# A two-layer diffusion backbone on one core: gate transposes by DMA in the later FFNs, and two modulation streams at other times and rates

## The chip, the cores and the metric

The program runs on one core of a Trainium2 chip. TensorE (PE) multiplies, VectorE (DVE), ScalarE (ACT) and GpSimd (POOL) work on tiles in on-chip memory, SyncE (SP) issues nearly all transfers. The metric is the device time of one execution in microseconds, as the median of several runs. One execution of the kernel was recorded by the hardware profiler; all rows quoted here are from it.

## What is computed

The program runs two layers over 256 latent tokens and 256 context tokens of width 1024, in float32. Each layer is a gated FFN of half weight, a mixer and another such FFN; the mixer is neighbourhood attention in layer 0 and a short gated convolution in layer 1. Each sub-layer has a shift, a scale and a gate from a modulation vector, a product of the conditioning vector with `ada_w`.

```python
def swiglu_ffn(h, w_in, w_out):
    a, u = jnp.split(h @ w_in, 2, axis=-1)        # w_in: 1024 x 5632
    return (jax.nn.silu(a) * u) @ w_out           # w_out: 2816 x 1024

def half_step_ffn(x, shift, scale, gate, w_in, w_out, g, b):
    y = swiglu_ffn(modulate(x, shift, scale), w_in, w_out)
    return post_norm_update(x, y, gate, 0.5, g, b)   # layer_norm(alpha*x + 0.5*gate*y)

m = (s_c @ ada_w[i] + ada_b[i]).reshape(B, N_MOD, 1, D)   # nine vectors per layer
```

After the attention only the latent tokens go on. What is left then is the second FFN of layer 0, written FFN(0,1), then FFN(1,0), the convolution (products `wc` and `wo`), and FFN(1,1). These three FFNs are where the change works.

## The kernel before

**Products.** Every matrix is split in a high part, rounded to the float32r type, and a low part that holds the rest. A product is then three matmuls: high by high and high by low (lines 165 and 166 of the kernel, in `mmu`), low by high (line 168). One call of `mmu` takes two 128-row blocks of the contraction, so six matmuls with 512 columns. The text calls it a chunk. After each chunk `tick` moves a clock on by one, and everything that is put off is counted in these chunks.

**Weights.** `wunit` loads 512 KB of weights (a unit) into one of four raw buffers on SP's queue. ScalarE rounds it to the high part (line 211, in two halves) and VectorE subtracts to the low part (line 214, in two halves). There are five buffers for the high part and five for the low part, and in the last phase `ext[0]` more of each, from tags `whx` and `wlx`: three, so eight in all.

**w1 of an FFN.** `panels` runs over 11 panels of 256 gate and 256 up columns. A panel has four units and two token tiles of 128 tokens, eight chunks. The end of a token tile's panel is `gated.done`: ScalarE applies silu (line 494), VectorE multiplies by the up half (line 495, tile `sil`). Four chunks later (`Late(G_LAG, rest)`) TensorE transposes the two token tiles' results in four 128x128 pieces into a PSUM tile `gT` (line 503), and `finish` splits that into `gh` on ScalarE (line 113) and `gl` on VectorE (line 114). These are the left operands of w2.

**w2 of an FFN.** `out_gemm` goes through 22 units (11 for each half of the 1024 output columns). `order_skew` lets the second token tile follow the first by `LEAD` = 5 units, so in the steady part each unit of progress is two chunks. At the end of each output tile the residual and the norm's statistics run on VectorE (lines 402 to 409).

**Modulation streams.** `stream` and `ada` produce the vectors that later sub-layers need, in the background: 16 steps for two vectors, each step one 512 KB load `ar` (line 316) and, one step later, an addition on VectorE in two halves (tile `acc`, line 297; the first step of a vector is a plain product). The additions are held behind the last gate multiplication that was issued (`gate_ins`). When a vector's eight steps are done, GpSimd adds over the partitions (line 307) and a small accumulating DMA adds the sum into a scratch row in memory (line 308). Later SP loads such rows as `mrow` (line 376), which waits for that DMA. `set_background(gen, rate, hold)` emits `rate` steps per chunk after `hold` chunks; `drain` emits what is left at once, at the place in the program where it stands. The name (1, 4) below is vector 4 of layer 1.

**What sets the order.** TensorE's order is that of the program text. The other engines' orders are planned from it when the program is built. On every engine instructions run in their queue's order. In FFN(0,1) the stream for (1,4) and (1,5) runs beside w1 at 0.35 after 20 chunks, in FFN(1,0) that of (1,6) and (1,7) at 0.25 from the start, and both are drained after w1. In FFN(1,1) and the weights around it a stream of one vector, (1,8), runs at 0.15.

Of the kernel before, what the change touches and what calls it, by code (L numbers as in the profile page):

```python
# [9 lines left out]

F32 = mybir.dt.float32
F32R = mybir.dt.float32r
AF = mybir.ActivationFunctionType
ALU = mybir.AluOpType
AX = mybir.AxisListType
# [2 lines left out]
P = 128  # L18
# [7 lines left out]
NP = FF // 256  # L26
# [26 lines left out]
LT_LAG = (5, 5)  # L53
F0_LAG = (5, 5, 6, 7)
G_LAG = 4
ROPE_EARLY = 70
S_EARLY = 40
V_LAG = 1
# [3 lines left out]
W_HI = 2  # L62
# [2 lines left out]
ZP = ((0, 0), (1, 0), (0, 1), (0, 2), (1, 1), (1, 2))  # L65
E0 = (0,)
E2 = (0, 5, 7)
HOLD = 20


@with_exitstack
def backbone_kernel(
# [6 lines left out]
    nc = tc.nc  # L79
    sync = nc.sync  # L80
# [4 lines left out]
    sp = ctx.enter_context(tc.tile_pool(name="sp", bufs=2))  # L85
# [4 lines left out]

    uid = [0]
    w_early = [0]
    ext = [1, 0]
    ada_late = [0]

    def nm(s):
        uid[0] += 1
        return f"{s}_{uid[0]}"
# [54 lines left out]
    def set_background(gen, rate, hold=0):  # L153

        background[:] = [gen, rate, -rate * hold]

    def drain():
        while background[0] is not None:
            bg_step()
# [20 lines left out]
    def wunit(srcs, kn, s, own=None, wd=512, put_off=False):  # L180

        raw = wp.tile([P, UN], F32, tag="wr", bufs=WB[0], name=nm(s + "r"))
        if own:
            hs, ls = ([act(F32R, s + c) for _ in range(kn)] for c in "hl")
            rv = raw[:, :kn * 512].rearrange("p (a b) -> p a b", a=kn)
            with tc.high_priority(offset=w_early[0]):
                for src, c in srcs:
                    sync.dma_start(rv[:, :, c:c + src.shape[2]], src)  # L190
                for i in range(kn):
                    with queued(own[i]):
                        nc.scalar.activation(hs[i], rv[:, i], AF.Copy)
                        nc.vector.tensor_tensor(out=ls[i], in0=rv[:, i], in1=hs[i].bitcast(F32), op=ALU.subtract)
            return Parts(hs), Parts(ls)
        ext[1] += 1
        if ext[0] and ext[1] % (5 + ext[0]) in (E0 if ext[0] == 1 else E2):
            hi = hp.tile([P, UN], F32R, tag="whx", bufs=ext[0], name=nm(s + "h"))
            lo = hp.tile([P, UN], F32R, tag="wlx", bufs=ext[0], name=nm(s + "l"))
        else:  # L200
            hi = wp.tile([P, UN], F32R, tag="wh", bufs=WB[1], name=nm(s + "h"))
            lo = wp.tile([P, UN], F32R, tag="wl", bufs=WB[2], name=nm(s + "l"))
        rv, hv, lv = (t[:, :kn * wd].rearrange("p (a b) -> p a b", a=kn) for t in (raw, hi, lo))
        with tc.high_priority(offset=w_early[0]):
            for src, c in srcs:
                sync.dma_start(rv[:, :, c:c + src.shape[2]], src)

        def parts():
            m = kn * wd
            for a in range(0, m, m // W_HI):  # L210
                nc.scalar.activation(hi[:, a:a + m // W_HI], raw[:, a:a + m // W_HI], AF.Copy)  # L211
            for a in range(0, m, m // W_LO):
                b = a + m // W_LO
                nc.vector.tensor_tensor(out=lo[:, a:b], in0=raw[:, a:b], in1=hi[:, a:b].bitcast(F32), op=ALU.subtract)  # L214
            return hv, lv

        if put_off:
            return parts
        with tc.high_priority(offset=w_early[0]):
            return parts()  # L220
# [131 lines left out]
    def stream(*groups):  # L352
        for g in groups:
            yield from ada(g)
            made[0] += 1
            if made[0] == ADA_SLOW:
                background[1] = ADA_FAST
# [100 lines left out]
    def lead_in(np):  # L458

        r = range(KU)  # L460
        o = [(0, 0, u) for u in r] + [(0, 1, u) for u in r[:2]] + [(1, 0, u) for u in r] + [(1, 1, u) for u in r[:2]]
        o += [(t, 1, u) for u in r[2:] for t in range(2)]
        return o + [(t, p, u) for p in range(2, np) for u in r for t in range(2)]
# [20 lines left out]
    def run(gen):  # L484
        for _ in gen:
            pass

    def gated(func, finish, s):

        part, res = {}, []  # L490

        def done(p, t, bk):
            g = sp.tile([P, 256], F32, tag="s2", bufs=S2, name=nm("sil"))
            nc.scalar.activation(g, bk[:, 0:256], func)
            gate_ins[:] = [nc.vector.tensor_tensor(out=g, in0=g, in1=bk[:, 256:512], op=ALU.mult)]
            part[p, t] = g
            if t == 1:
                def rest():
                    ps = tpb(s)
                    for i in range(2):  # L500
                        g = part.pop((p, i))
                        for j in range(2):
                            nc.tensor.transpose(ps[:, j * 256 + i * P:j * 256 + (i + 1) * P], g[:, j * P:(j + 1) * P], ident)  # L503
                    return finish(p, ps)
                res.append(Late(G_LAG, rest))

        return done, res
# [325 lines left out]
    def lhs_T(tl):  # L833
        def f(k, t):
            s = (k % 2) * 256 + t * P
            g = tl[k // 2]
            hi, lo = g.get() if isinstance(g, Late) else g
            return hi[:, s:s + P], lo[:, s:s + P]
        return f

    def ffn(hTs, later, l, j, i, gm, nxt, own=()):
        def finish(p, ps):
            hi, lo = act(F32R, "gh"), act(F32R, "gl")
            split(ps, hi, lo)
            return hi, lo

        done, gT = gated(AF.Silu, finish, "gT")

        def done2(p, t, bk):
            done(p, t, bk)  # L850
            if p == 1 and t == 1:
                later()

        run(panels([(p * 256, FF + p * 256) for p in range(NP)], ffn_w_in[l, j], hTs, lead_in(NP), done2, "w1", own))
        drain()
        g, hTs, later = sub_end(ffn_w_out[l, j], lhs_T(gT), 2 * NP, l, i, gm, 0.5, nxt, "w2",
                                order_skew(NP) if nxt else order_last(NP))
        run(g)
        return hTs, later
# [263 lines left out]
    hp = phase.__enter__()  # L1123
    on_pool[0] = True
    sync.dma_start(scr[1][0, 4 * D:9 * D].rearrange("(a b) -> a b", a=16), ada_b[1, 4 * D:9 * D].rearrange("(a b) -> a b", a=16))
    ext[0] = 3

    set_background(stream([(1, 4, 0), (1, 5, 0)]), 0.35, HOLD)
    hTs, later = ffn(hTs, later, 0, 1, 2, 8, (1, 0), own)

    set_background(stream([(1, 6, 0), (1, 7, 0)]), 0.25)
    hTs, later = ffn(hTs, later, 1, 0, 0, 2, (1, 3))


    srow = cp.tile([24, P], F32, tag="row", name="srow")
# [52 lines left out]

    cols = [(0, 256), (512, 768)] + [(D + n * 256, 2 * D + n * 256) for n in range(4)]
    run(panels(cols, w, hTs, lead_in(6), done, "wc"))  # L1190
    g, hTs, later = sub_end(sc_w_out[0], lhs_T(yT), KC, 1, 1, 5, 1.0, (1, 6), "wo", order_late(KU))
    run(g)
    set_background(stream([(1, 8, 0)]), 0.15)
# [55 lines left out]
```

## Time and profile before

| | |
|---|---|
| median of three runs | 1257.53 us (1256.62 to 1257.73) |
| the profiled execution | 1258.45 us, of which the span of its records is 1256.7 us |
| mean granted TensorE clock | 0.998 |
| TensorE busy | 1241.4 us, 99% of the span |
| VectorE busy | 966.5 us, 77% |
| ScalarE busy | 590.2 us, 47% |

The stages can be told from the matmuls' operands. All times are in us from the span's start; the shares are worked out from one row per stage of a view by windows.

| stage | from, to | TensorE | VectorE | ScalarE | DMA share |
|---|---|---|---|---|---|
| FFN(0,0), both kinds of tokens | 0, 320 | 99% | 79% | 30% | 0.81 |
| attention | 320, 591 | 99% | 79% | 57% | 0.52 |
| FFN(0,1) w1 | 591, 718 | 99% | 88% | 58% | 0.87 |
| FFN(0,1) w2 | 718, 780 | 100% | 54% | 41% | 0.51 |
| FFN(1,0) w1 | 780, 906 | 100% | 87% | 57% | 0.82 |
| FFN(1,0) w2 | 906, 968 | 100% | 54% | 41% | 0.52 |
| convolution, wc and wo | 968, 1062 | 100% | 81% | 55% | 0.62 |
| FFN(1,1) w1 | 1062, 1188 | 99% | 78% | 58% | 0.71 |
| FFN(1,1) w2, end | 1188, 1256 | 90% | 53% | 27% | 0.38 |

How to read the rows in the next part: a timeline row has the start, the duration, the engine, the kernel's line, the operation, the tile written and those read, shapes, and in brackets how long the engine was idle before and what released it. In a row of groups the busy time and the mean in ns come after the first bar, the idle time and its releasers after the second. A row of waits has the waiting line, the releaser, the total in us, the count and the longest. SPq is SyncE's queue. `DMA share` is the mean busy share of 16 DMA engines.

### The profile page before, as it was taken

The numbers are of one execution on the slowest core, as the hardware profiler recorded it, in microseconds if no ns is written. First come the engines' busy times: TensorE is split into PE (matmuls) and PEld (weight loads), VectorE is DVE, ScalarE is ACT, GpSimd is POOL, SyncE is SP. The second block draws the span as 40 slices with busy tenths as digits, with TensorE's granted clock in tenths as the row PEclk, the third lists the DMA queues.
The fourth block names the chain that finished last, engine by engine and source line by source line (L and its number), as shares of the span: only waits on it lengthen the run. The fifth ranks groups of instructions, "written<-read, shape, count | busy, mean of one in ns | idle before, by whom it ended". The sixth has DMA issues, their size and how long they took to land.

```text
span 1256.7 us, 17284 instructions
## 1 busy us (share of the span) xinstructions
PE 1241.4 (99%) x5902; PEld 1006.9 (80%) x5902; DVE 966.5 (77%) x1675; ACT 590.2 (47%) x1152; POOL 85.0 (7%) x83
## 2 busy tenths in 40 slices
PE   8999999999999999999999999999999999999997
PEld 6787778778878878777888888888888887888886
DVE  3599987888878877789899646998646788878546
ACT  2432132312326556688655435655435744655431
POOL 0000000000001111120003100021100000002000
PEclk9999999999999999999999999999999999999999
DMA  9976678788842744455899645889645764885641
GB/s 308 299 235 226 197 236 290 265 260 274 285 156 85 216 94 87 99 115 179 259 335 318 231 150 167 274 293 321 224 146 167 245 206 134 259 290 185 227 159 53
DMA packets 202928, 268.59 MB, mean 214 GB/s; under 512 B 30246, under 2 KB 149534, under 8 KB 202840
## 3 DMA queue, kind: packets, MB, share of 16 engines
q1 hardware_dynamic: 202644, 267.46, 67.4%
q8 instruction: 46, 0.75, 0.2%
q14 instruction: 42, 0.34, 0.1%
q0 software_dynamic: 160, 0.02, 0.0%
q10 hardware_dynamic: 36, 0.02, 0.0%
HBM read 265.27 MB, written 2.20 MB: 213 GB/s over the span
## 4 chain that ended last, share of the span: by engine, by line
PE 92%; ACT 3%; DVE 3%; issue 1%; DMA 1%; POOL 0%; DVEq 0%; SPq 0%; POOLq 0%; ACTq 0%
PE f L695 19%; PE w L165 17%; PE w L168 17%; PE w L166 17%; PE wkv L165 2%; PE wkv L166 2%; PE wkv L168 2%; PE wc L165 2%; PE wc L168 2%; PE wc L166 2%; PE gT L503 1%; PE ada L624 1%; PE hT L437 1%; PE S L987 1%; PE wo L165 1%
## 5 line engine op out<-in xcount | busy, mean ns | idle before, releaser
L211 ACT ACTIVATE w1h<-w1r 128x512 fp32r<-128x512 f32 (+1 forms) x352 | 200.0, 620 | 180.0 <-PE w L168 81.5
L214 DVE TENSOR_TENSOR w1l<-w1r,w1h 128x512 fp32r<-128x512 f32 (+1 forms) x352 | 241.7, 734 | 35.5 <-ACT w1h L211 33.2
L165 PE MATMUL w<-w1h,hTh 128*128 128x512 f32 x528 | 209.1, 396 | 1.3 <-ACT hTh L113 1.3
L166 PE MATMUL w<-w1l,hTh 128*128 128x512 f32 x528 | 205.9, 390 | 0.3 <-DVE w1l L214 0.3
L297 DVE SCALAR_TENSOR_TENSOR acc<-ar,cst,acc 128x512 f32<-128x512 f32 x266 | 186.2, 747 | 15.3 <-DMA ar<-in_ada_w_dram 15.3
L165 PE MATMUL w<-w2h,gh 128*128 128x512 f32 (+1 forms) x446 | 173.4, 389 | 0.0
L166 PE MATMUL w<-w2l,gh 128*128 128x512 f32 (+1 forms) x446 | 172.1, 387 | 0.0
L211 ACT ACTIVATE w2h<-w2r 128x512 fp32r<-128x512 f32 x176 | 101.5, 624 | 145.2 <-PE w L168 106.5
L214 DVE TENSOR_TENSOR w2l<-w2r,w2h 128x512 fp32r<-128x512 f32 x176 | 114.1, 688 | 72.0 <-ACT w2h L211 71.2
L168 PE MATMUL w<-w1h,hTl 128*128 128x512 f32 x528 | 163.1, 390 | 0.2 <-DVE hTl L114 0.2
L168 PE MATMUL w<-w2h,gl 128*128 128x512 f32 (+1 forms) x446 | 136.1, 386 | 0.0
L695 PE MATMUL f<-h0h,w1h 128*128 128x512 f32 x352 | 133.1, 394 | 0.4 <-DVE h0h L650 0.4
L695 PE MATMUL f<-h0l,w1h 128*128 128x512 f32 x352 | 133.2, 391 | 0.0
L695 PE MATMUL f<-h0h,w1l 128*128 128x512 f32 x352 | 132.7, 390 | 0.0
L165 PEld LDWEIGHTS w<-w1h,hTh 128*128 128x128 f32 x528 | 99.2, 188 | 21.8 <-ACT hTh L113 2.1
L168 PEld LDWEIGHTS w<-w1h,hTl 128*128 128x128 f32 x528 | 98.9, 188 | 22.0 <-DVE hTl L114 1.0
L166 PEld LDWEIGHTS w<-w1l,hTh 128*128 128x128 f32 x528 | 99.2, 188 | 20.4 <-DVE w1l L214 0.7
L165 PEld LDWEIGHTS w<-w2h,gh 128*128 128x128 f32 x446 | 83.8, 188 | 19.3 <-issue 1.7
L166 PEld LDWEIGHTS w<-w2l,gh 128*128 128x128 f32 x446 | 83.8, 188 | 16.6
L168 PEld LDWEIGHTS w<-w2h,gl 128*128 128x128 f32 x446 | 83.3, 188 | 17.1
L695 PEld LDWEIGHTS f<-h0h,w1h 128*128 128x128 f32 x352 | 65.7, 188 | 19.0 <-issue 4.2
L695 PEld LDWEIGHTS f<-h0l,w1h 128*128 128x128 f32 x352 | 65.5, 188 | 14.4 <-issue 0.8
(189 smaller groups left out, 1719.6 us busy)
## 6 DMA issues: line engine op xcount, KB each, us to landing
w1r<-in_ffn_w_in_dram SPq DMA_DIRECT2D x340, 256.0 KB
ar<-in_ada_w_dram SPq DMA_DIRECT2D x128, 512.0 KB
w2r<-in_ffn_w_out_dram SPq DMA_DIRECT2D x88, 512.0 KB
ar<-in_ada_w_dram SPq DMA_DIRECT2D x32, 256.0 KB
wkvr<-in_na_w_qkv_dram SPq DMA_DIRECT2D x32, 256.0 KB
wcr<-in_sc_w_in_dram SPq DMA_DIRECT2D x32, 256.0 KB
wqr<-in_na_w_qkv_dram SPq DMA_DIRECT2D x8, 512.0 KB
wor<-in_na_w_out_dram SPq DMA_DIRECT2D x8, 512.0 KB
```

Source lines behind the costliest of these rows:

```text
L165: nc.tensor.matmul(ps, lh, rh, start=first and i == 0, stop=False)
L166: nc.tensor.matmul(ps, lh, rl, start=False, stop=False)
L168: nc.tensor.matmul(ps, ll, rh, start=False, stop=last and i == n - 1)
L211: nc.scalar.activation(hi[:, a:a + m // W_HI], raw[:, a:a + m // W_HI], AF.Copy)
L214: nc.vector.tensor_tensor(out=lo[:, a:b], in0=raw[:, a:b], in1=hi[:, a:b].bitcast(F32), op=ALU.subtract)
L297: nc.vector.scalar_tensor_tensor(out=a, in0=src, scalar=sc, in1=a, op0=ALU.mult, op1=ALU.add)
L437: nc.tensor.transpose(ps[:, k * P:(k + 1) * P], z[h][:, k * P:(k + 1) * P], ident)
L503: nc.tensor.transpose(ps[:, j * 256 + i * P:j * 256 + (i + 1) * P], g[:, j * P:(j + 1) * P], ident)
L624: nc.tensor.matmul(ps[o:o + 32, 0:m], cst[:, a * kt + i, :], w[:, i, j, :], start=(a == 0 and i < 2), stop=(a == last and i >= kt - 2))
L695: nc.tensor.matmul(ps, w, hT0[k][part == 1], start=(k == part == 0), stop=(k == KC - 1 and part == 1))
L987: nc.tensor.matmul(banks[i], (qh, qh, ql)[f][ps, qs], (kh, kl, kh)[f][ps, :], start=f == 0, stop=f == 2)
```

## The change

In the three later FFNs panels 0 to 8 of the 11 no longer go through TensorE for the transpose. Each token tile's gate result is taken as 16-bit halves of its 32-bit words. ScalarE copies it apart into a tile of low halves and high halves (`hal`, 128x512 of 16 bits). A DMA transpose on SP's queue turns that into half of the panel's tile `halT`. Twenty-two chunks later (`D_LAG`) ScalarE joins the halves again into a float32 tile `gTw`, placed behind the weight rounding that was issued last (`last_split`), and `finish` splits that as before. Panels 9 and 10 stay on TensorE with a lag of 4.

The stream for (1,4) and (1,5) begins after 60 chunks at 0.3, and is drained behind w2 of FFN(0,1); the one for (1,6) and (1,7) begins after 80 chunks at 0.22, and is drained behind the convolution's `wc`. The extra weight buffers go from three to two, so seven in all.

```diff
--- before.py
+++ after.py
@@ -10,6 +10,7 @@
 
 F32 = mybir.dt.float32
 F32R = mybir.dt.float32r
+U16 = mybir.dt.uint16
 AF = mybir.ActivationFunctionType
 ALU = mybir.AluOpType
 AX = mybir.AxisListType
@@ -53,6 +54,8 @@
 LT_LAG = (5, 5)
 F0_LAG = (5, 5, 6, 7)
 G_LAG = 4
+D_LAG = 22
+BY_DMA = NP - 2
 ROPE_EARLY = 70
 S_EARLY = 40
 V_LAG = 1
@@ -65,7 +68,7 @@
 ZP = ((0, 0), (1, 0), (0, 1), (0, 2), (1, 1), (1, 2))
 E0 = (0,)
 E2 = (0, 5, 7)
-HOLD = 20
+HOLD = 60
 
 
 @with_exitstack
@@ -90,6 +93,7 @@
 
     uid = [0]
     w_early = [0]
+    last_split = []
     ext = [1, 0]
     ada_late = [0]
 
@@ -208,7 +212,7 @@
         def parts():
             m = kn * wd
             for a in range(0, m, m // W_HI):
-                nc.scalar.activation(hi[:, a:a + m // W_HI], raw[:, a:a + m // W_HI], AF.Copy)
+                last_split[:] = [nc.scalar.activation(hi[:, a:a + m // W_HI], raw[:, a:a + m // W_HI], AF.Copy)]
             for a in range(0, m, m // W_LO):
                 b = a + m // W_LO
                 nc.vector.tensor_tensor(out=lo[:, a:b], in0=raw[:, a:b], in1=hi[:, a:b].bitcast(F32), op=ALU.subtract)
@@ -485,7 +489,7 @@
         for _ in gen:
             pass
 
-    def gated(func, finish, s):
+    def gated(func, finish, s, by_dma=0):
 
         part, res = {}, []
 
@@ -493,6 +497,22 @@
             g = sp.tile([P, 256], F32, tag="s2", bufs=S2, name=nm("sil"))
             nc.scalar.activation(g, bk[:, 0:256], func)
             gate_ins[:] = [nc.vector.tensor_tensor(out=g, in0=g, in1=bk[:, 256:512], op=ALU.mult)]
+            if p < by_dma:
+                if t == 0:
+                    part[p] = hp.tile([P, 4, 256], U16, tag="halT", bufs=3, name=nm("halT"))
+                halves = hp.tile([P, 2, 256], U16, tag="hal", bufs=2, name=nm("hal"))
+                nc.scalar.activation(halves, g.bitcast(U16).rearrange("p (f s) -> p s f", s=2), AF.Copy)
+                sync.dma_start_transpose(part[p][:, :, t * P:(t + 1) * P], halves.rearrange("p s f -> p (s f)"))
+                if t == 1:
+                    def joined():
+                        w = sp.tile([P, 512], F32, tag="tmp", bufs=3, name=nm("gTw"))
+                        with queued(last_split):
+                            nc.scalar.activation(w.bitcast(U16).rearrange("p (f s) -> p s f", s=2),
+                                                 part.pop(p).rearrange("p (s j) n -> p s (j n)", s=2), AF.Copy)
+                        return finish(p, w)
+
+                    res.append(Late(D_LAG, joined))
+                return
             part[p, t] = g
             if t == 1:
                 def rest():
@@ -838,13 +858,13 @@
             return hi[:, s:s + P], lo[:, s:s + P]
         return f
 
-    def ffn(hTs, later, l, j, i, gm, nxt, own=()):
+    def ffn(hTs, later, l, j, i, gm, nxt, own=(), made_here=True):
         def finish(p, ps):
             hi, lo = act(F32R, "gh"), act(F32R, "gl")
             split(ps, hi, lo)
             return hi, lo
 
-        done, gT = gated(AF.Silu, finish, "gT")
+        done, gT = gated(AF.Silu, finish, "gT", BY_DMA)
 
         def done2(p, t, bk):
             done(p, t, bk)
@@ -852,7 +872,8 @@
                 later()
 
         run(panels([(p * 256, FF + p * 256) for p in range(NP)], ffn_w_in[l, j], hTs, lead_in(NP), done2, "w1", own))
-        drain()
+        if made_here:
+            drain()
         g, hTs, later = sub_end(ffn_w_out[l, j], lhs_T(gT), 2 * NP, l, i, gm, 0.5, nxt, "w2",
                                 order_skew(NP) if nxt else order_last(NP))
         run(g)
@@ -1123,13 +1144,14 @@
     hp = phase.__enter__()
     on_pool[0] = True
     sync.dma_start(scr[1][0, 4 * D:9 * D].rearrange("(a b) -> a b", a=16), ada_b[1, 4 * D:9 * D].rearrange("(a b) -> a b", a=16))
-    ext[0] = 3
-
-    set_background(stream([(1, 4, 0), (1, 5, 0)]), 0.35, HOLD)
-    hTs, later = ffn(hTs, later, 0, 1, 2, 8, (1, 0), own)
-
-    set_background(stream([(1, 6, 0), (1, 7, 0)]), 0.25)
-    hTs, later = ffn(hTs, later, 1, 0, 0, 2, (1, 3))
+    ext[0] = 2
+
+    set_background(stream([(1, 4, 0), (1, 5, 0)]), 0.3, HOLD)
+    hTs, later = ffn(hTs, later, 0, 1, 2, 8, (1, 0), own, False)
+    drain()
+
+    set_background(stream([(1, 6, 0), (1, 7, 0)]), 0.22, HOLD + 20)
+    hTs, later = ffn(hTs, later, 1, 0, 0, 2, (1, 3), (), False)
 
 
     srow = cp.tile([24, P], F32, tag="row", name="srow")
@@ -1188,6 +1210,7 @@
 
     cols = [(0, 256), (512, 768)] + [(D + n * 256, 2 * D + n * 256) for n in range(4)]
     run(panels(cols, w, hTs, lead_in(6), done, "wc"))
+    drain()
     g, hTs, later = sub_end(sc_w_out[0], lhs_T(yT), KC, 1, 1, 5, 1.0, (1, 6), "wo", order_late(KU))
     run(g)
     set_background(stream([(1, 8, 0)]), 0.15)
```

TensorE, in the middle of w1 of FFN(0,1), before: `w` are the PSUM tiles of the two token tiles, `w1h` and `w1l` the weights' parts, `hTh` and `hTl` the activations' parts, and `gT` the transposed gate.

```order
L166 MATMUL w_1136_6085<-w1l_6106,hTh_5710 128x512
L168 MATMUL w_1136_6085<-w1h_6105,hTl_5711 128x512 x2
L503 MATMUL gT_6119<-ident,sil_6062 128x128 x2
L503 MATMUL gT_6119<-ident,sil_6073 128x128 x2
L165 MATMUL w_1137_6092<-w1h_6105,hTh_5806 128x512
L166 MATMUL w_1137_6092<-w1l_6106,hTh_5806 128x512
```

The same engine after the change, around the same panel's second half; line numbers are four higher there.

```order
L169 MATMUL w_1120_5994<-w1h_6044,hTh_5824 128x512
L170 MATMUL w_1120_5994<-w1l_6045,hTh_5824 128x512
L172 MATMUL w_1120_5994<-w1h_6044,hTl_5825 128x512 x2
L169 MATMUL w_1138_6086<-w1h_6078,hTh_5710 128x512
L170 MATMUL w_1138_6086<-w1l_6079,hTh_5710 128x512
L169 MATMUL w_1138_6086<-w1h_6078,hTh_5710 128x512
```

The two rows of L503 are gone, and the chunks follow each other directly.

SP, in w1 of FFN(0,1) after the change: `w1r` are raw weight tiles, loaded in two pieces each.

```order
L210 DMA w1r_6287<-in_ffn_w_in_dram 128x2x256 [waits DMAHW4_49,DMAHW3_49,DVE_49]
L210 DMA w1r_6287<-in_ffn_w_in_dram 128x2x256
L210 DMA w1r_6310<-in_ffn_w_in_dram 128x2x256 [waits DMAHW5_49,DMAHW6_49,DVE_49,Activation_49]
L505 DMA_TRANSPOSE halT_6061<-hal_6062 128x4x128 [waits Activation_49]
L505 DMA_TRANSPOSE halT_6061<-hal_6074 128x4x128 [waits DMAHW7_49,Activation_49]
L210 DMA w1r_6310<-in_ffn_w_in_dram 128x2x256 [waits DMAHW0_49]
L210 DMA w1r_6331<-in_ffn_w_in_dram 128x2x256 [waits DMAHW1_49,DVE_49]
```

Two transposes per panel have come between the weight loads; each waits for ScalarE, and the weight loads of later panels stand behind it.

VectorE from the last gate multiplications of w1 on, before: `sil` is the gate result, `w2l` the low parts of w2, `gl` the low part of the transposed gate, `gcol` columns of the next sub-layer's modulation.

```order
L495 TENSOR_TENSOR sil_6943<-sil_6943,w_1288_6863 128x256
L495 TENSOR_TENSOR sil_6952<-sil_6952,w_1289_6870 128x256
L214 TENSOR_TENSOR w2l_7094<-w2r_7092,w2h_7093 128x512 x2
L114 TENSOR_TENSOR gl_7013<-gT_7007,gh_7012 128x512
L382 COPY gcol_7060<-mcT_7058 128x32
L383 SCALAR_TENSOR_TENSOR gcol_7060<-gcol_7060 128x8
L384 SCALAR_TENSOR_TENSOR gcol_7060<-gcol_7060 128x8
L385 TENSOR_TENSOR gcol_7060<-gcol_7060 128x8
L214 TENSOR_TENSOR w2l_7114<-w2r_7112,w2h_7113 128x512 x2
```

The same place after the change, from the last addition of vector (1,4) on; the last gate multiplication and one weight pair stand right ahead of it.

```order
L301 SCALAR_TENSOR_TENSOR acc_6644<-ar_6930,cst,acc_6644 128x512 x2
L299 TENSOR_SCALAR acc_7068<-ar_6981,cst 128x512 x2
L118 TENSOR_TENSOR gl_7008<-gT_7002,gh_7007 128x512
L118 TENSOR_TENSOR gl_7042<-gTw_7039,gh_7041 128x512
L301 SCALAR_TENSOR_TENSOR acc_7068<-ar_7066,cst,acc_7068 128x512 x2
L301 SCALAR_TENSOR_TENSOR acc_7068<-ar_7098,cst,acc_7068 128x512
L386 COPY gcol_7061<-mcT_7059 128x32
L301 SCALAR_TENSOR_TENSOR acc_7068<-ar_7098,cst,acc_7068 128x512
L387 SCALAR_TENSOR_TENSOR gcol_7061<-gcol_7061 128x8
L388 SCALAR_TENSOR_TENSOR gcol_7061<-gcol_7061 128x8
L301 SCALAR_TENSOR_TENSOR acc_7068<-ar_7136,cst,acc_7068 128x512
L218 TENSOR_TENSOR w2l_7104<-w2r_7102,w2h_7103 128x512 x2
```

Additions of the stream (`acc`) now stand around the two `gl` and the `gcol` rows, ahead of the weight pair `w2l_7104`; before there were none at this place.

SP, before, in w1 of FFN(0,1), where `mrow` is the load of modulation rows from the scratch that GpSimd's DMA (the semaphore DMASW0) writes:

```order
L206 DMA w1r_6776<-in_ffn_w_in_dram 128x2x256 [waits DMAHW3_49,DVE_49]
L206 DMA w1r_6776<-in_ffn_w_in_dram 128x2x256 [waits DMAHW4_49]
L376 DMA mrow_8707<-scr_117 8x128 [waits DMAHW5_49,DMASW0_49]
L206 DMA w1r_6806<-in_ffn_w_in_dram 128x2x256 [waits DMAHW6_49,DVE_49]
L206 DMA w1r_6806<-in_ffn_w_in_dram 128x2x256 [waits DMAHW7_49]
L316 DMA ar_6601<-in_ada_w_dram 128x1024 [waits DMAHW0_49,DVE_49]
L316 DMA ar_6629<-in_ada_w_dram 128x1024 [waits DMAHW1_49,DVE_49]
```

After the change the same load stands in w2, among the stream's last loads:

```order
L320 DMA ar_7098<-in_ada_w_dram 128x1024 [waits DMAHW5_49,DVE_49]
L320 DMA ar_7136<-in_ada_w_dram 128x1024 [waits DMAHW6_49,DVE_49]
L320 DMA ar_7185<-in_ada_w_dram 128x1024 [waits DMAHW7_49,DMAHW3_49,DVE_49]
L380 DMA mrow_8702<-scr_117 8x128 [waits DMAHW0_49,DMASW0_49]
L320 DMA ar_7216<-in_ada_w_dram 128x1024 [waits DMAHW5_49,DMAHW1_49,DVE_49]
L380 DMA mrow_9977<-in_ln_g_dram 8x128 [waits DMAHW2_49,PE_49]
L210 DMA w2r_7195<-in_ffn_w_out_dram 128x2x512 [waits DVE_49]
L320 DMA ar_7254<-in_ada_w_dram 128x1024 [waits DMAHW6_49,DMAHW4_49,DVE_49]
L210 DMA w2r_7220<-in_ffn_w_out_dram 128x2x512 [waits DVE_49]
```

Behind `mrow` there are now four loads of the stream and the rest of w2's weight units, beginning with `w2r_7195`.

## The prediction

> **What bounds the kernel now.** I read the page's busy shares and its chain first, and then what TensorE waits for in the part that the change touches (700 to 1250 us).
>
> ```profile
> PE 1241.4 (99%) x5902; PEld 1006.9 (80%) x5902; DVE 966.5 (77%) x1675; ACT 590.2 (47%) x1152; POOL 85.0 (7%) x83
> PE 92%; ACT 3%; DVE 3%; issue 1%; DMA 1%; POOL 0%; DVEq 0%; SPq 0%; POOLq 0%; ACTq 0%
> PE w L165 <- ACT hTh L113: 0.7, 1, 0.7
> PE w L168 <- DVE hTl L114: 0.2, 1, 0.2
> ```
>
> TensorE works 99% of the span and 92% of the chain is its own. From 700 us to 1250 us its data waits are the last two rows: 0.9 us. So time falls only where instructions leave TensorE, and rises only where another engine makes it wait. The slack of the others differs by stage.
>
> ```profile
> core 0: us, PE busy (x) PEld busy (x) DVE busy (x) ACT busy (x) POOL busy (x), PEclk, DMA share, GB/s
> 605.00:660.00 55.00, 55.00 (x254) 45.51 (x253) 49.40 (x85) 31.32 (x60) 2.76 (x1) 1.00 0.92 303
> 730.00:776.00 46.00, 46.00 (x205) 38.09 (x204) 27.52 (x45) 19.71 (x35) 1.12 (x2) 1.00 0.57 183
> 1162.00:1186.00 24.00, 24.00 (x111) 19.85 (x110) 13.74 (x23) 11.76 (x23) 0.00 (x0) 1.00 0.59 194
> ```
>
> The first row is w1 of FFN(0,1) with the old modulation stream beside it: DMA 0.92, VectorE 49.4 of 55. The second is w2 of the same FFN without a stream: VectorE has 40% free. The third is w1 of FFN(1,1) after its stream has ended: DMA 0.59.
>
> **What leaves TensorE.** Two chunks follow, then the place where four transposes stand.
>
> ```profile
> 700.05 0.48 PE L165 MATMUL w<-w1h,hTh 128*128 128x512 f32 x1
> 701.53 0.39 PE L165 MATMUL w<-w1h,hTh 128*128 128x512 f32 x1
> 702.89 0.39 PE L165 MATMUL w<-w1h,hTh 128*128 128x512 f32 x1
> ...
> 710.60 0.62 PE L168 MATMUL w<-w1h,hTl 128*128 128x512 f32 x2
> 711.06 0.60 PE L503 MATMUL gT<-ident,sil 128*128 128x128 f32 x4
> 711.41 0.48 PE L165 MATMUL w<-w1h,hTh 128*128 128x512 f32 x1
> 711.73 0.40 PE L166 MATMUL w<-w1l,hTh 128*128 128x512 f32 x1
> ```
>
> A chunk takes 1.36 us (701.53 to 702.89). From one group's successor to the next (700.05 to 711.41) are 11.36 us, and eight chunks are 10.88, so one panel's four transposes cost 0.48. At the place itself they take 0.35 (711.06 to 711.41), and the first matmul behind them 0.32 instead of 0.23: 0.44. I take the middle, 0.46. Three FFNs with nine panels each give 27 × 0.46 = **12.4 us less**. That comes in full only if every weight is still there in time.
>
> ```profile
> L503 PE MATMUL gT<-ident,sil x132: 270/272/330, 611.5 to 1192.9; 128*128 128x128 f32 x132
> ```
>
> The median duration of 272 ns agrees with the Trainium skill ("TensorE: Matmul & The Clock Gate", Part 4), which gives about 275 ns for such a transpose in context. By that price 108 of them would be 29.4 us; the starts above decide, since neighbouring instructions overlap.
>
> **What the new path costs.** ScalarE gets two copies and a join per panel, and VectorE keeps its subtraction. The rows of ScalarE in this w1 (605 to 706 us):
>
> ```profile
> L211 ACT ACTIVATE w1h<-w1r 128x512 fp32r<-128x512 f32 x72 | 41.5, 625 | 30.8 <-PE w L168 14.3 <-DMA w1r<-in_ffn_w_in_dram 11.5 <-DVE acc L297 2.8
> ```
>
> A copy of 512 elements is 0.62 us, the join of 1024 an estimated 1.24, together 2.5 us in 10.9. With its 31.3 of 55 us ScalarE would be at 80%. Its largest idle is for buffers that TensorE has not freed, which shows that weights run ahead of their use. I charge nothing; the cover is that idle of 30.8 us, three per panel. Without it, 27 × 2.5 = 67 us would be at stake.
>
> The 54 DMA transposes (128 KB each) have no row. They share SP's queue with the weights, and each waits there for ScalarE's copy, with up to seven weight units queued behind. The nearest rows:
>
> ```profile
> q1 hardware_dynamic: 202644, 267.46, 67.4%
> L206 SPq DMA_DIRECT2D w1r<-in_ffn_w_in_dram x20: 367/415/465, 1131.2 to 1157.5; - x20
> ```
>
> At the 303 GB/s of the first window 128 KB are 0.43 us. A packet holds an engine 66.9 ns on the mean (0.674 × 16 × 1256.7 us / 202,644); 512 pieces of 256 bytes on 16 engines would be 2.1 us, and single elements, 65,536 of them, 274 us each. DMA is used to 0.59 without a stream, so two transposes may fill 0.41 × 10.9 us: 2.2 each. SP would allow (10.9 − 8 × 0.415) / 2 = 3.8 each to issue. I take a value between 0.43 and 2.1, since the transpose reads runs of 1 KB as the weight loads do: hidden. Above 2.2, each further us costs 54.
>
> A rule of the Trainium skill speaks against this edit: "VectorE: DVE Perf Modes", The three transpose paths, gives TensorE 390 ns and the DMA crossbar 1309 ns for 128x128 two-byte elements, and its rules prefer TensorE. Four blocks would be 5.2 us, an estimate from that page, and if they cannot overlap the sum would rise by 54 × (5.2 − 2.2) = 162. Another page of the Trainium skill, "DMA: Bandwidth & Descriptors", Latency and other measured facts, has 261 GB/s, which makes 0.5 us. No run of before can decide; the rival below has its own price.
>
> **What the later streams and the lost buffer cost.** The hi/lo weight buffers go from eight to seven. Steady w2 before:
>
> ```profile
> 739.64 0.39 PE L165 MATMUL w<-w2h,gh 128*128 128x512 f32 x1
> 739.85 1.15 ACT L211 ACTIVATE w2h<-w2r 128x512 fp32r<-128x512 f32 x2 [1.57 <-PE w L168]
> 740.51 1.29 DVE L214 TENSOR_TENSOR w2l<-w2r,w2h 128x512 fp32r<-128x512 f32 x2 [1.43 <-ACT w2h L211]
> ...
> 743.16 0.69 DVE L409 BATCH_NORM_STATS2 st<-x 128x6 f32<-128x512 f32 x1
> 743.77 1.28 DVE L214 TENSOR_TENSOR w2l<-w2r,w2h 128x512 fp32r<-128x512 f32 x2
> 745.09 0.39 PE L165 MATMUL w<-w2h,gh 128*128 128x512 f32 x1
> 745.31 0.39 PE L166 MATMUL w<-w2l,gh 128*128 128x512 f32 x1
> ```
>
> TensorE frees a buffer at 739.8, its lo half is done at 741.80, and L166 needs it at 745.31: 3.5 us of slack. A unit lasts two chunks, 2.72 us, so with one buffer fewer 0.8 remains, and 0.3 where the residual rows stand between. Before, that is covered: VectorE is idle for 1.4 us ahead of each pair. After, the streams' additions stand in that place. VectorE works in order, and the accumulate is held until the last gate, so the additions stand ahead of the weight pairs:
>
> ```profile
> 718.35 0.39 PE L165 MATMUL w<-w2h,gh 128*128 128x512 f32 x1
> 718.96 0.42 DVE L495 TENSOR_TENSOR sil<-sil,w 128x256 f32<-128x256 f32 x1 [0.84 <-ACT sil L494]
> 719.48 1.30 DVE L214 TENSOR_TENSOR w2l<-w2r,w2h 128x512 fp32r<-128x512 f32 x2
> 723.69 0.69 DVE L114 TENSOR_TENSOR gl<-gT,gh 128x512 fp32r<-128x512 f32 x1 [2.91 <-ACT gh L113]
> ...
> 729.61 1.29 DVE L214 TENSOR_TENSOR w2l<-w2r,w2h 128x512 fp32r<-128x512 f32 x2 [1.58 <-ACT w2h L211]
> L297 DVE SCALAR_TENSOR_TENSOR acc<-ar,cst,acc 128x512 f32<-128x512 f32 x28 | 19.5, 744 | 0.0
> 876.11 7.68 POOL L307 PARTITION_ALL_REDUCE red<-acc  x1 [34.41 <-DVE acc L297]
> 884.08 0.79 POOL L308 DMA_DIRECT2D scr<-red  x1 [0.29 <-POOL red L307]
> 887.81 0.30 SPq L376 DMA_DIRECT2D mrow<-scr  x1
> ```
>
> I run the new order of VectorE from 718.35 as zero: gate 1.04; a weight pair 2.43; additions 7 to 11 with two gl, 1.49 per pair and 0.69 per gl, to about 11; the next pair 11.3 to 12.6 (needed 13.4, in time); two more additions; the third pair ends at 16.2, needed at 16.1 (stall 0.1 to 0.2). SP meanwhile stands at the mrow row, which needs the reduction of vector 4. The last rows above give 11.7 us from the reduction's start to that row (876.1 to 887.8); its addition ends at 4.0, so SP goes on at 15.7, and only then loads the rest of the stream and unit 11 of w2. The next load lands at an estimated 18.5 (2.8 later, 1.7 of it for 512 KB at 303 GB/s), its addition ends at 20.0 and the pair behind it at 21.3, needed at 19.0: stall 2.3. The next two, one load apart, stall 0.8 and 1.5. Together **4.8 us** (between 1, if the loads run ahead, and 8, if each waits in turn).
>
> In w2 of FFN(1,0) seven units in a row carry an addition each: 2 × 0.69 + 2 × 0.747 = 2.87 us of VectorE per unit of 2.72, 0.15 each, plus 0.8 at the residual: about **2.0** (0.5 to 4). In w2 of FFN(1,1) nothing competes: 0.3. The conv's products have no such density; I take nothing there.
>
> **Sum.** The profiled execution took 1258.45 us (span 1256.7 and 1.8 around it): 1258.45 − 12.4 + 4.8 + 2.0 + 0.3 = 1253.1. It lay 0.9 above the median of 1257.53, so I say **1252.2**; with stalls of 3 to 9 us, 1249 to 1255.
>
> **The rivals.**
> *All hidden.* The 12.4 come whole, as when the additions slip behind the weights because their loads land late: 1257.5 − 12.4 = 1245. For it: the stalls are differences of tenths against sums of many rows. Against it: the in-order VectorE queue, and SP's stand at mrow.
> *Stalls about double.* If the loads behind the mrow row come in turn with w2's weights, 10 to 14 us of stall give 1255 to 1260: no difference that can be told.
> *Slower, by the transposes.* If one holds the DMA rings or SP's queue for more than 2.2 us, weights come late in every panel; it outweighs the gain of the forecast from 0.1 us above that (5.3 / 54). At 2.4 each, 54 × 0.2 = 10.8 us: 1263, and open above. For it: every weight load stands behind the transposes in one queue, and the upper bound by packets, 2.1, is next to the threshold. Against it: those are pieces of 256 bytes at a mean taken over larger ones. The crossbar price quoted from the Trainium skill above would be this case.
> *The change does not do what it says* (TensorE does not gain the 0.46): the starts around 711 speak against it, since nothing but the transposes stands there.
>
> **How the numbers follow.** A measurement of this kernel can tell about 0.2%, 2.5 us, from no change. Forecast (1249 to 1255) 0.42; all hidden 0.20; stalls double 0.15; slower by the transposes 0.21; the change without effect, either way, 0.02. Faster 0.42 + 0.20 + 0.01 = 0.63, same 0.15, slower 0.22. The range 1244 to 1263 leaves out a part of the slower case, some 0.15, and little below.
>
> **What would show it.** The starts of L165 one panel apart in w1: 10.88 instead of 11.36. In w1 no TensorE wait for w1h or w1l; one there in every panel is the slower rival. In w2 of FFN(0,1) waits for w2l of some us, with SP waiting at mrow from about 725 us less the gain so far; none is the all-hidden rival. A transpose's packets longer than 2.2 us in sum, or a DMA share near 1 in w1 without a stream, would make the prediction wrong, and so would w2 stalls over 10 us.

## The result, and the profile after

The kernel after takes 1265.92 us (median of 4 runs, 1264.08 to 1266.92) against 1257.63 for the kernel before: ratio of the means 1.0063, 95% interval 1.0046 to 1.0081. It is slower, where 1252.2 was forecast with a range of 1244 to 1263. The profiled execution took 1264.99 us, its span is 1263.2.

First the stages, from the first matmul of a stage to that of the next, in us of the two profiled executions:

| stage | before | after | difference |
|---|---|---|---|
| FFN(0,1) w1 | 126.2 | 121.6 | −4.6 |
| FFN(0,1) w2 | 61.8 | 71.6 | +9.8 |
| FFN(1,0) w1 | 126.2 | 121.1 | −5.1 |
| FFN(1,0) w2 | 61.9 | 70.9 | +9.1 |
| convolution | 94.5 | 95.6 | +1.1 |
| FFN(1,1) w1 | 125.8 | 121.3 | −4.5 |
| FFN(1,1) w2, end | 68.2 | 68.6 | +0.5 |

The differences are taken before rounding. The three w1 bring 14.2 us and the first two w2 take 18.9. The profile page's busy line, the waits of TensorE from 590 us on (waiting line, releaser, us in total, times, longest), and windows over w1 and w2 of FFN(0,1), then of FFN(1,0), in the kernel after:

```profile
PE 1234.9 (98%) x5794; PEld 998.3 (79%) x5794; DVE 967.7 (77%) x1675; ACT 645.8 (51%) x1233; POOL 79.2 (6%) x83
PE w L170 <- DVE w2l L218: 11.8, 7, 4.9
592.50:714.00 121.50, 121.48 (x540) 100.22 (x541) 90.10 (x156) 89.44 (x164) 1.07 (x2) 1.00 0.94 268
714.00:785.50 71.50, 65.68 (x278) 51.49 (x278) 54.74 (x80) 27.30 (x51) 15.82 (x7) 0.95 0.68 228
785.70:906.70 121.00, 121.00 (x541) 100.19 (x540) 81.65 (x140) 88.48 (x162) 1.08 (x2) 1.00 0.88 235
906.80:977.60 70.80, 64.72 (x278) 51.63 (x277) 57.60 (x90) 27.38 (x51) 8.23 (x4) 0.95 0.77 255
```

A window has its ends, its length, the busy time of PE, PEld, DVE, ACT and POOL, the granted clock, the DMA share and GB/s. In w1 TensorE does not wait for weights: the transposes are hidden, as forecast, and ScalarE is 74% busy there (89.44 of 121.5 us). In both w2 the weights' low half comes late from VectorE, and the granted clock falls to 0.95. What VectorE does there stands in its timeline of w2 of FFN(0,1), with GpSimd's rows of the same time:

```profile
717.92 5.16 DVE L299 TENSOR_SCALAR acc<-ar,cst 128x512 f32<-128x512 f32 x2
718.26 6.13 POOL L311 PARTITION_ALL_REDUCE red<-acc  x1 [120.67 <-DVE acc L301]
...
740.71 0.68 DVE L218 TENSOR_TENSOR w2l<-w2r,w2h 128x512 fp32r<-128x512 f32 x1
740.90 6.47 POOL L311 PARTITION_ALL_REDUCE red<-acc  x1 [15.06 <-DVE acc L301]
741.31 0.68 DVE L406 SCALAR_TENSOR_TENSOR res<-w,gate 128x512 f32<-128x512 f32 x1
741.91 4.42 DVE L218 TENSOR_TENSOR w2l<-w2r,w2h 128x512 fp32r<-128x512 f32 x1
```

The half of a weight pair that takes 0.68 us at 740.71 takes 4.42 at 741.91, while GpSimd adds over the partitions. TensorE's timeline at this place:

```profile
741.78 0.40 PE L169 MATMUL w<-w2h,gh 128*128 128x512 f32 x1
746.39 0.80 PE L170 MATMUL w<-w2l,gh 128*128 128x512 f32 x1 [4.21 <-DVE w2l L218]
746.98 1.05 PE L172 MATMUL w<-w2h,gl 128*128 128x512 f32 x2
747.84 0.63 PE L169 MATMUL w<-w2h,gh 128*128 128x512 f32 x1
748.26 0.63 PE L170 MATMUL w<-w2l,gh 128*128 128x512 f32 x1
748.69 0.63 PE L169 MATMUL w<-w2h,gh 128*128 128x512 f32 x1
...
750.77 0.40 PE L170 MATMUL w<-w2l,gh 128*128 128x512 f32 x1
751.00 0.40 PE L169 MATMUL w<-w2h,gh 128*128 128x512 f32 x1
751.24 0.39 PE L170 MATMUL w<-w2l,gh 128*128 128x512 f32 x1
```

The matmul of 741.78 is followed by the next at 746.39, 4.6 us later. From there to 750.4 matmuls start 0.43 us apart instead of 0.23, which costs another 2.1 us. A window over that stretch has a granted clock of 0.50:

```profile
743.90:750.70 6.80, 4.31 (x10) 3.44 (x11) 4.83 (x5) 0.07 (x1) 4.27 (x2) 0.50 0.40 124
```

In w2 of FFN(1,0) the same happens at 929 us, with 5.3 us and then rows at half rate. There the long instructions are two products of the stream, right ahead of the weight pair:

```profile
927.44 6.13 POOL L311 PARTITION_ALL_REDUCE red<-acc  x1 [137.01 <-DVE acc L301]
928.42 5.44 DVE L299 TENSOR_SCALAR acc<-ar,cst 128x512 f32<-128x512 f32 x2 [1.11 <-DMA ar<-in_ada_w_dram]
934.50 0.79 PE L170 MATMUL w<-w2l,gh 128*128 128x512 f32 x1 [4.87 <-DVE w2l L218]
```

These two places make 13 to 14 of the 18.9 us.

The long instructions were there before. This is one of five places, the reduction that the prediction quotes at 876.11 (7.68 us); `x4` are four halves of weights:

```profile
875.92 1.89 DVE L214 TENSOR_TENSOR w1l<-w1r,w1h 128x512 fp32r<-128x512 f32 x3
877.72 0.68 DVE L114 TENSOR_TENSOR gl<-gT,gh 128x512 fp32r<-128x512 f32 x1
878.33 6.23 DVE L214 TENSOR_TENSOR w1l<-w1r,w1h 128x512 fp32r<-128x512 f32 x4
```

Four halves would be 2.5 us (1.89 for three); they take 6.23. Before, all five reductions fell in a w1, where weights run far ahead. The means of the groups had shown it as well: from 605 to 706 us L214 takes 789 ns on `w1l` and 689 ns on `w2l`, for the same operation and shape.

### The profile page after: what moved, and what is told of

Read it like the earlier page. It is cut to its first block, busy times and chain, and to the rows that moved or that the text cites. A ratio compares the mean times of both kernels' runs of the same rounds, so it can differ in the third digit from the quotient of the medians.

```text
span 1263.2 us, 17255 instructions
## 1 busy us (share of the span) xinstructions
PE 1234.9 (98%) x5794; PEld 998.3 (79%) x5794; DVE 967.7 (77%) x1675; ACT 645.8 (51%) x1233; POOL 79.2 (6%) x83
## 4 chain that ended last, share of the span: by engine, by line
PE 85%; DVE 6%; ACT 3%; DMA 3%; issue 2%; POOL 0%; DVEq 0%; SPq 0%; ACTq 0%; POOLq 0%
PE f L715 19%; PE w L170 16%; PE w L169 16%; PE w L172 16%; DMA ar<-in_ada_w_dram 2%; PE wkv L169 2%; PE wkv L170 2%; PE wkv L172 2%; PE wc L169 2%; PE wc L170 2%; PE wc L172 2%; DVE w2l L218 1%; DVE acc L301 1%; PE hT L441 1%; PE ada L644 1%
## 5 line engine op out<-in xcount | busy, mean ns | idle before, releaser
L218 DVE TENSOR_TENSOR w1l<-w1r,w1h 128x512 fp32r<-128x512 f32 (+1 forms) x352 | 228.1, 692 | 58.2 <-ACT w1h L215 56.3
L169 PE MATMUL w<-w1h,hTh 128*128 128x512 f32 x528 | 206.2, 391 | 1.2 <-ACT hTh L117 1.2
L301 DVE SCALAR_TENSOR_TENSOR acc<-ar,cst,acc 128x512 f32<-128x512 f32 x266 | 186.5, 746 | 19.0 <-DMA ar<-in_ada_w_dram 18.9
L170 PE MATMUL w<-w2l,gh 128*128 128x512 f32 (+1 forms) x446 | 175.3, 394 | 11.9 <-DVE w2l L218 11.8
L218 DVE TENSOR_TENSOR w2l<-w2r,w2h 128x512 fp32r<-128x512 f32 x176 | 118.0, 708 | 53.1 <-ACT w2h L215 52.3
L715 PEld LDWEIGHTS f<-h0l,w1h 128*128 128x128 f32 x352 | 65.5, 188 | 14.3 <-issue 0.6
```

Of the source, the lines that this page charges most:

```text
L169: nc.tensor.matmul(ps, lh, rh, start=first and i == 0, stop=False)
L170: nc.tensor.matmul(ps, lh, rl, start=False, stop=False)
L301: nc.vector.scalar_tensor_tensor(out=a, in0=src, scalar=sc, in1=a, op0=ALU.mult, op1=ALU.add)
L715: nc.tensor.matmul(ps, w, hT0[k][part == 1], start=(k == part == 0), stop=(k == KC - 1 and part == 1))
```

## The experiments

Each is compared with the kernel before, run on the same chip; e1 to e11 are the names of the runs. Theory A, formed from the rows above: each of GpSimd's sums holds an instruction of VectorE for some 4 to 5 us; the change moves two of them into w2 of FFN(0,1) and one into that of FFN(1,0), where one instruction of that length exceeds what the weights are ahead.

**Sums left out (e1).**

```diff
-            red = hp.tile([P, D], F32, tag="red", name=nm("red"))
-            nc.gpsimd.partition_all_reduce(red, acc[i], P, ReduceOp.add)
+            red = acc[i]
```

The kernel leaves out the addition over the partitions, so its modulation vectors are not complete.

> The kernel after, with GpSimd's sums over the partitions left out (the small DMA takes row 0 of the accumulator, so the modulation vectors of layer 1 from 4 on are not complete). Theory A (in w2 each of GpSimd's sums holds VectorE: single instructions of 4.4 to 5.4 us at 718, 742 and 928 us; then TensorE starves, and runs at half clock for some 4 us): these long instructions go, w2 of FFN(0,1) falls from 71.6 to 64-66 us, w2 of FFN(1,0) from 70.9 to 63-65, together 12 to 15 us: 1251 to 1254. Theory B (the additions that stand ahead of the weight pairs and the stream's late loads make the waits; the long instructions are wrongly drawn or beside the point): both w2 stay above 68, 1261 to 1266.

1250.99 us, ratio 0.9946 (0.9931 to 0.996). The w2 are 62.8 and 67.4 us. VectorE at the same place, with the same additions around it:

```profile
718.42 0.87 DVE L299 TENSOR_SCALAR acc<-ar,cst 128x512 f32<-128x512 f32 x2
```

The pair of products that took 5.16 us there takes 0.87 now. GpSimd's small DMA is still there, and SP stands at `mrow` for 2.3 us here against 1.1 after, so neither makes the long instructions. Theory A accounts for most of the loss: the two w2 fall by 8.9 and 3.5 us, which is 12.3 of the 12.4 us between the two profiled executions. The medians differ by 14.9, since the profiled execution of this run is its slowest and that of the kernel after lies under its median. Theory A does not account for all: the second w2, at 67.4, is well above the 63 to 65 that theory A gave and keeps 5.6 us over before, in waits of 0.5 to 1.4 us each, without a long instruction. Additions in a row and late loads stand there; the run with spaced additions below bears on them.

**Streams as before (e2).** The two lines of the streams with 0.35 after 20 chunks and 0.25 from the start, drained after w1; all else as after.

> The kernel after, with the streams at the old times and rates (0.35 after 20 chunks, 0.25 from the start, both drained after w1). Theory A and B: both w2 fall to 62 to 62.5 us, 18 us less than after. In w1 the DMA share was 0.92 without a stream's loads, and 16 loads of 1.7 us each would make 139 us of DMA work in a stage of 121, less some 15 us that the weights run ahead: 0 to 8 us of waits per w1. Total 1248 to 1262, the spread being those waits. Theory C (the transposes themselves delay w2, not the streams): w2 stays above 68 us, 1264 or more.

1274.47 us, ratio 1.0136 (1.0119 to 1.0153). The w2 are 61.8 and 63.3, as expected, so the lost buffer and the transposes alone do not slow w2. But w1 takes 135.8 and 132.6 us, some 14 and 11 more than after, where at most 8 were expected; the time is outside the expected range. So with the streams at their old times the transposes cost more than they save.

**Streams alone (e3).** `gated(AF.Silu, finish, "gT")` without the last argument: all panels on TensorE, the rest as after.

> The kernel after without the DMA transposes: all panels on TensorE with a lag of 4, the new streams, seven weight buffers. If the two parts add (A and B): w1 as before (126), both w2 as after (71.6 and 70.9): 1257.6 + 18.9 + 1 = 1275 to 1279. Theory C: both w2 below 66, under 1266.

1275.08 us, ratio 1.0135 (1.012 to 1.015). The w2 are 72.8 and 69.4: the two parts of the change add, as expected, and w2 loses as much without the transposes.

**One vector per w1 (e5).** (1,4) at 0.13 in the first w1, (1,5) at 0.13 in the second, each drained there, (1,6) and (1,7) at 0.4 in the convolution.

> The kernel after with the same loads at other places: vector (1,4) alone beside w1 of FFN(0,1), (1,5) alone beside w1 of FFN(1,0), each at 0.13 and drained there, and (1,6) and (1,7) beside the convolution at 0.4. Theory A: no sum of GpSimd's falls in a w2, so w2 of FFN(0,1) is 62 to 63 us; that of FFN(1,0) 62 to 65, as additions may still stand at its start; w1 stays at 121 to 122 since 8 loads add 0.11 to the DMA share: 1245 to 1250, faster than before. Theory B: w2 of FFN(1,0) stays above 67, the total near 1252 to 1256.

1256.94 us, ratio 0.999 (0.9981 to 0.9999): a miss. The w2 are 61.8 and 63.7 as theory A has it, but the convolution takes 106.1 instead of 95.6: TensorE waits 6.2 us for a gate product of VectorE at two places. The longer wait, at 1039 us, stands at a sum (1037 to 1043 us). The other, at 1012, comes 8 us behind a sum's end, while VectorE is busy for 19.1 of 20 us. How much the sums do there, and how much the 16 additions beside a busy VectorE, was not separated.

**Eight buffers (e4).** The streams alone, with `ext[0] = 3`.

> The streams alone (no DMA transposes), but with eight weight buffers instead of seven. Theory A with the buffers as cushion: each unit is ready 2.7 us earlier, so the two long waits for weights in w2 (4.2 and 4.9 us with seven buffers) shrink to about 1.5 and 2.2, the small ones go, and the rows at half clock behind them go where the wait is under some 2 us: w2 of FFN(0,1) 63 to 65 instead of 72.8, of FFN(1,0) 63 to 66 instead of 69.4; total 1262 to 1266. Rival D (the buffer has no part in it): both as with seven, 1273 to 1276.

1270.36 us, ratio 1.0097 (1.0082 to 1.0112). w2 of FFN(1,0) falls from 69.4 to 65.2: its long wait is 1.9 us there instead of 4.9, and no rows at half rate follow. w2 of FFN(0,1) falls by 1.5 only, to 71.3, where 63 to 65 was expected, and the total misses its range too. Two sums 24 us apart and the bunched additions probably use up the cushion before the second sum comes; that was not tried.

**Seven buffers alone (e6).** The kernel before with `ext[0] = 2`.

> The kernel before with seven weight buffers instead of eight, nothing else. All theories but one: nothing stands in w2, so the 0.8 us that remain suffice: w2 61.8 to 62.1, total within 1 us of before. Rival D' (the lost buffer costs by itself, since GpSimd's sums fall in w1 and w1 too has less to run ahead): 1260 to 1264.

1257.97 us, ratio 0.9999 (0.999 to 1.0009), w2 61.9 both times. The buffer costs nothing as long as nothing disturbs w2.

**Additions spaced (e8).** Each addition is placed behind the low half of the weights that was issued last.

```diff
-                for i in gate_ins:
+                for i in gate_ins + (last_lo if on_pool[0] else []):
```

> The kernel after, with each addition of a stream held behind the weight pair that was issued last, so that additions stand one by one between the pairs and not in a row ahead of them. Loads, rates and drains as in after. Theory A: GpSimd's sums still fall in w2, two or three of them, so one or two long waits of 4 to 5 us with half clock behind them stay; the short waits go: 1256 to 1263. Theory B (the order of the additions is the cause): both w2 at 62 to 63: 1246 to 1250.

1257.85 us, ratio 0.9996 (0.9987 to 1.0006). The w2 are 66.8 and 67.4, 8.3 us less than after in the two. The short waits for weights are gone, one long one per w2 is left, at a sum again:

```profile
753.70 0.69 DVE L407 SCALAR_TENSOR_TENSOR res<-w,gate 128x512 f32<-128x512 f32 x1
754.30 4.67 DVE L219 TENSOR_TENSOR w2l<-w2r,w2h 128x512 fp32r<-128x512 f32 x1
```

Leaving out the sums takes 12.3 us off the two w2, spacing the additions 8.3: together more than the loss of 18.9. So part of the loss needs both, a lead used up by the additions and then a sum.

**Paced: sums in w1 and in the convolution (e7).** Spaced additions, and one vector behind the other at rates that put the sums elsewhere.

```diff
+    def paced(*groups):
+        for rate, g in groups:
+            background[1] = rate
+            yield from ada(g)
...
-    set_background(stream([(1, 4, 0), (1, 5, 0)]), 0.3, HOLD)
+    set_background(paced((0.13, [(1, 4, 0)]), (0.105, [(1, 5, 0)]), (0.22, [(1, 6, 0)]), (0.1, [(1, 7, 0)])), 0.13)
```

> Additions held as in e8, and the vectors one behind the other so that GpSimd's sums fall in w1 or in the middle of the convolution: (1,4) at 0.13 in w1 of FFN(0,1), (1,5) at 0.105 through w2 into w1 of FFN(1,0), (1,6) at 0.22 in that w1, (1,7) at 0.1 through w2 into the convolution. Theory A: no long instruction of VectorE in w2, additions one at a time fit into its idle 1.4 us per unit: both w2 at 61.9 to 62.5, w1 at 121.1 to 122, convolution 94 to 97: total 1244 to 1248, faster than both kernels. Theory B, or a buffer too few: w2 stays at 64 or above with additions alone, 1250 or more.

1246.64 us (1246.08 to 1246.76), ratio 0.9908 (0.9893 to 0.9923): faster than both kernels. Windows over w1 and w2 of FFN(0,1), then of FFN(1,0):

```profile
592.10:713.70 121.60, 121.58 (x540) 100.28 (x541) 96.54 (x160) 89.34 (x164) 8.73 (x5) 1.00 0.93 283
713.80:775.60 61.80, 61.80 (x279) 50.74 (x278) 41.24 (x71) 27.49 (x52) 1.12 (x2) 1.00 0.64 209
775.60:897.40 121.80, 121.56 (x541) 100.12 (x540) 102.51 (x163) 87.34 (x162) 17.25 (x8) 1.00 0.95 283
897.50:959.30 61.80, 61.80 (x279) 50.74 (x278) 41.93 (x70) 27.54 (x52) 1.12 (x2) 1.00 0.64 211
```

TensorE is busy throughout both w2, at the full granted clock, with additions of (1,5) and (1,7) beside it (ten halves in each). One sum falls at 811 us in w1, and the pairs there take 6.68 us for four halves without a wait on TensorE:

```profile
811.19 6.13 POOL L312 PARTITION_ALL_REDUCE red<-acc  x1 [30.14 <-DVE acc L302]
811.40 6.68 DVE L219 TENSOR_TENSOR w1l<-w1r,w1h 128x512 fp32r<-128x512 f32 x4 [0.35 <-ACT w1h L216]
```

**Paced streams alone (e9).** The same without DMA transposes.

> e7 without the DMA transposes: all panels on TensorE, streams paced and additions spaced as in e7, seven buffers. It prices the transposes alone. If the paced streams cost and bring nothing: every stage as in before, 1257 to 1259, so that e7's gain is the transposes', 27 panels at 0.42 to 0.5 us. If the new order of the streams is itself faster than the old one: 1250 to 1254.

1262.86 us, ratio 1.0033 (1.0021 to 1.0046): not as expected. The w2 are 61.8 both times, but the second w1 is 130.3 us. TensorE's and VectorE's rows:

```profile
816.22 5.30 DVE L219 TENSOR_TENSOR w1l<-w1r,w1h 128x512 fp32r<-128x512 f32 x2
821.44 0.41 DVE L500 TENSOR_TENSOR sil<-sil,w 128x256 f32<-128x256 f32 x1
...
821.90 0.44 PE L524 MATMUL gT<-ident,sil 128*128 128x128 f32 x2 [2.32 <-DVE sil L500]
```

A sum holds VectorE just ahead of the gate product, which a transpose on TensorE needs four chunks later. With the DMA transposes the product is not needed until 22 chunks later, and the same sum costs no wait in e7. The first and third w1, where no sum makes TensorE wait, are 4.33 us longer than in e7 (126.0 against 121.67, 125.62 against 121.30): 0.48 per panel of nine.

**Transposes from ScalarE's queue (e10).** e2 again, to see whether its w1 is slow because SP stands at the transposes (33.6 us in the first w1).

> e2 (DMA transposes with the streams at the old times) with the transposes issued from ScalarE's queue in place of SP's. Theory S (in e2 SP stands at a transpose, 33.6 us in w1 of FFN(0,1), with the weight loads behind it): SP no longer waits for ScalarE's copy, w1 falls from 136 and 133 us to 121-126: 1246 to 1256. Theory F (the DMA engines are full with transposes, 16 loads and the weights): w1 stays at 130 or more, 1268 or more. A third outcome: ScalarE, 75% busy in w1 and with 1.2 us more per transpose, becomes the bound: waits for w1h on TensorE, in between.

1275.37 us, ratio 1.0132 (1.0117 to 1.0147); w1 136.9 and 133.7. So SP's stand at the transposes is not what makes w1 long by itself. From 620 to 700 us the DMA share is 1.00:

```profile
620.00:700.00 80.00, 79.75 (x350) 64.94 (x348) 66.78 (x107) 51.67 (x92) 7.46 (x2) 1.00 1.00 293
```

A share of 1.00 is not a limit that was shown: TensorE is busy for 79.75 of these 80 us, and in the kernel after the share is 1.14, at 317 GB/s, from 1130 to 1150 us without a wait of TensorE.

**Old streams without sums (e11).** e2 with the edit of e1.

> e2 (DMA transposes, streams at the old times) with GpSimd's sums left out as in e1. If w1 of e2 is slow because the DMA engines are full: w1 stays at 130 us or more, 1264 to 1274. If it is slow because the sums hold VectorE while the weights have lost their lead: w1 121 to 124, total 1244 to 1250. Between the two (DMA takes the lead away, the hold turns that into the wait): 124 to 130, 1250 to 1264.

1271.09 us, ratio 1.0108 (1.0091 to 1.0125); w1 130.9 and 132.1 in the profiled execution, the fastest of its four. ScalarE's waits from 640 to 723 us:

```profile
ACT w1h L215 <- DMA w1r<-in_ffn_w_in_dram: 18.8, 9, 4.9
```

Without any sum 9 and 11 us of e2's 14 and 11 over the kernel after stay, so the sums are not the main cause there. The row shows weights that land late. Why they do stays open: in e2 the DMA share from 620 to 700 us is 0.89, at 271 GB/s, less than the 303 GB/s that the prediction's first window shows before. The records of the DMA packets give the transposes' own part: in the trace of the kernel after each transpose is 512 packets of 256 bytes, which last 26 ns on the mean, so 0.84 us of 16 engines (22 ns and 0.71 in e2).

## Why the prediction was wrong

- **TensorE's gain.** Forecast 12.4 us, 0.46 per panel. In the kernel after the three w1 lose 14.2, 0.53 per panel; e7 against e9 gives 0.48 where only the transposes differ. The term was right, slightly small. The 275 ns of the Trainium skill ("TensorE: Matmul & The Clock Gate", Part 4), set beside the median of 272, is for two-byte elements; here they have four bytes, so that agreement carries little.
- **ScalarE and the DMA transposes hidden.** Right: no wait for weights in w1 after. Sizes were off. The join is 1.36 us, not 1.24, and a transpose occupies SP's queue for 1.19 us, within the 3.8 that the prediction allowed. ScalarE's idle time of 30.8 us was only for 14.3 us a wait for buffers, and for 11.5 us one for loads, so the cover was smaller than the prediction read it. The transpose does not move runs of 1 KB, the reason given for a value below the upper bound: its packets are the 512 pieces of 256 bytes of that bound. They take 0.84 us and not 2.1, because a piece lasts 26 ns and not the mean of 66.9; that the result lay between the bounds was in part luck. In the second w1, where no stream loads, the DMA share is 0.92 against the 0.59 of the third window in the prediction. By the packet records 0.18 of it is the transposes' own, 0.92 us each in this window; the rest is weights at a higher rate and slower small packets. The threshold of 2.2 us took a share of 1 for the limit, which no run shows. These rows of the kernel after show the sizes:

```profile
L510 ACT ACTIVATE gTw<-halT x27: 1351/1362/1374, 626.6 to 1190.4; 128x1024 uint16<-128x1024 uint16 x27
L505 SPq DMA_TRANSPOSE halT<-hal x54: 1188/1195/2743, 602.9 to 1175.6; - x54
810.00:890.00 80.00, 80.00 (x355) 66.26 (x354) 51.34 (x88) 61.14 (x109) 0.00 (x0) 1.00 0.92 234
```

- **The two prices of the Trainium skill.** The crossbar price, an estimate of 5.2 us per transpose if blocks cannot overlap ("VectorE: DVE Perf Modes", The three transpose paths), does not hold here: 54 of them would have stalled w1, and no w1 waits for weights. The 0.5 us, an estimate from 261 GB/s ("DMA: Bandwidth & Descriptors", Latency and other measured facts) is too small beside the 0.84 of the packets.
- **The stalls of w2: the step that failed.** I forecast 4.8 and 2.0 us and measured 9.8 and 9.1. The stages and the queue were right (VectorE's pairs late, the additions ahead of them, 0.8 us of slack), the mechanism was only half there. I summed VectorE's order with each instruction at its undisturbed mean. What I left out is that GpSimd's sum stretches an instruction of VectorE by some 4 us, although the trace of before has five such cases, and the means of L214 differ by 100 ns for it. I took the reduction as a wait of SP at `mrow`; SP waited there only 1.1 us. e1 shows it: without the sums 12.3 us of both w2 go. What is left over before, 0.9 and 5.6, is together close to my 6.8 for additions and late loads, but that is luck: each of the two is off by some 4 us, in opposite directions. The prediction's own sign of being wrong, w2 stalls over 10 us, is the one that came.
- **The half clock.** Not in the forecast at all: some 2 us behind each long wait, 4 us for the two. The convolution, where I took nothing, is 1.1 us longer; its cause was not looked for.
- **The rivals.** "All hidden" gave 1245, and e7 reaches 1246.64 with the same parts in other places. "Slower" named the transposes; it came slower, by the streams. "Stalls double" had the place but stopped at 14 us; it was 18.9. The range ended at 1263, 3 us short.

## What to carry to other kernels

An operation on one engine can lengthen another engine's instructions. Compare the mean duration of the same operation and shape between groups, and look up the longest single instances before moving work from a stage with slack to one without. Place such operations where the stage runs ahead by more than they hold, and spread additions one by one: here the same work in other places and one by one is worth 19 us (1265.92 to 1246.64); the new places without the spacing were not tried. Freeing the engine that bounds the kernel is worth its full amount only while the engine that feeds it keeps its lead.

## What the runs showed of the hardware

- While GpSimd adds over the partitions (6.1 to 8.3 us, once 10.7 in e2), an instruction of VectorE that else takes 0.4 to 0.7 us lasts 2.2 to 5.0 us, 4.4 or more at 44 of the 55 sums in the traces. Each sum of every run has one; without the sums (e1, e11) no single data instruction of VectorE lasts over 1.3 us. The others beside a sum keep their usual length, as the 0.68 us of the residual row at 741.31 shows.
- Behind a break of TensorE, matmuls start 0.43 us apart instead of 0.23 for 3 to 5 us (7 to 12 rows in most cases). Breaks of 1.9 us and less between starts had no such rows behind them (1.3 after, 1.7 in e1, 1.8 in e5, 1.9 in e4), those of 2.6 and more had (2.6 in e9, 2.8 in e2, 4.6 after). At 2.3 to 2.4 both occur: in e5 rows at half rate follow, in e4 none. A break of 5 us so costs 7, an estimate from the two of the kernel after (4.6 and 2.1 more). What sets the limit was not tried by itself.
- A DMA transpose of 128x512 two-byte elements takes SP 1.19 us to issue, about three times a weight load's 0.42. It is moved in 512 packets of 256 bytes, of 26 ns each on the mean after.
